# Second layer's feed-forward as two phases over DRAM with seven half-block products (Strassen) in place of eight

## The chip, the cores and the metric

One core of a Trainium2 chip runs the whole kernel. The metric is the device time of one execution in microseconds, the median of several runs. Engines: TensorE (PE, with its weight loads PEld), VectorE (DVE), ScalarE (ACT), GpSimd (POOL) and SyncE (SP), which issues all transfers of the stage in question in the order of its list.

## What is computed

A model of two layers, on 1024 tokens of 1024 features with 256 tokens of context, all in float32. Layer 0 mixes by neighbourhood attention and a gated linear recurrence, layer 1 by gated linear attention and grouped-query attention. Each layer ends in a feed-forward of width 4096, modulated by a conditioning vector; the last layer needs it for the 1024 latent tokens alone:

```python
D_FF = 4 * D_MODEL
...
def squared_relu_mlp(u, w1, w2):
    return jnp.square(jax.nn.relu(u @ w1)) @ w2
```

with `u` the normed and modulated residual, and its result times a gate added to the residual; the last norm follows.

## The kernel before

Activations lie feature-major: 128 features on the partitions, tokens along the free axis, in two chunks of 512 (c = 0, 1). TensorE's products keep float32 accuracy by splitting every operand into hi + lo (a rounding cast by ScalarE, the rest by a subtraction on VectorE or GpSimd, `split`) and adding three matmuls, hi hi, hi lo, lo hi, into one PSUM bank (`mm3`, L131 to L133). A matmul is 128x128 stationary by 128x512 moving.

The stage is `ff` (L1304) called for layer 1 at L2138. `ff_ops` lists its products: (1, g, c) makes the hidden blocks of group g, two blocks of 128 of the 4096 hidden features, for chunk c, 8 input tiles each, so 48 matmuls; (2, g, c) multiplies them by their rows of w2 into all eight output tiles, again 48 matmuls. In all 2 x 32 blocks x 8 tiles x 3, that is 1536 matmuls for each of the two layers, 3072 together, 128 x 512 all but the last few. First- and second-layer products of neighbouring groups alternate, so hidden never leaves SBUF. The first ones are (1, 0, 0), (1, 1, 0), (2, 0, 0), (1, 0, 1): two groups of chunk 0, then a second-layer product, and only then chunk 1, whose norm is still going on (`norm_mod` L1222, `mod_part` L348: VectorE scales, L354, ScalarE shifts and casts, L355, and VectorE, L363, or GpSimd, L361, takes the lo).

Per hidden block ScalarE applies Relu from PSUM (L1344), GpSimd squares (L1345), ScalarE casts hi (L138), VectorE takes lo (L139). Per output tile VectorE adds gate times PSUM to the residual `hl` in SBUF (L1363). Weights come in units of 128x1024, 512 KB each, by SyncE, some units ahead (`w_load`, `w_ahead`): ScalarE casts hi (L90), GpSimd subtracts lo (L92). The last product is done in two halves of the tokens, woven with the last norm (`final`, L2023), the transposes for it (L2032) and the stores (L2046).

Every engine runs its own list in order: an instruction that waits holds up all behind it. The list is what the Python program emits; generators (`fills`, stepped by `tick`) put background work between the products. SBUF tiles come from a pool of 45 slots of 4 KB a partition (`E.S`), six temporaries (`E.T`, `f`, `t`) and eight PSUM banks (`E.P`).

Of the kernel before, what the change touches and what calls it, by code (L numbers as in the profile page):

```python
# [366 lines left out]
def start(E):  # L367
    """x, ctx: row sums of squares, transposes, modulation and the norm of layer 0; x.T goes to DRAM."""
# [78 lines left out]
def col_units(key, ap, c0, n):  # L447
    """n units of 128 columns of a [1024, *] weight."""
# [12 lines left out]
def tick(E):  # L461
    """One step of every background generator."""
# [5 lines left out]
def store(E, dst, src, lag=4):  # L468
    """A store that is issued some background steps later, when its data is there."""
# [12 lines left out]
def pipe(gens, gap):  # L482
    """Software pipeline: a generator starts every gap steps, all started ones advance by one per step."""
# [54 lines left out]
def lru_tile(E, j, xl, gl, ct, o_d):  # L538
    """Conv, gates, both recurrences and the output gate of channels 128 j .. 128 j + 127."""
# [87 lines left out]
def na_bias_setup(E):  # L627
    """rpb rows padded to 127 columns in DRAM, so that a [64, 64] Toeplitz block is one strided read."""
# [14 lines left out]
def na_head_load(E, h, qk_d, v_d):  # L643
    """Bias tables and operands of head h."""
# [31 lines left out]
def na_head_mask(E, hd, i):  # L676
    """Quarter i of the masks of a head's bias tables."""
# [84 lines left out]
def run_attention(E, units, fill=None, lag=3):  # L762
    """Software pipeline over the units of an iterator: norm 1, turn lag, values lag + 1 steps after the scores."""
# [30 lines left out]
def attn_out(E, pair, parity, dst, flip=False):  # L794
    """dst[64 rows at 64 * parity, two query tiles] = the four partial products of pair.ps [128, 2, 2, 128], times pair.r."""
# [16 lines left out]
class Pair:  # L812
    """The outputs of two query tiles in PSUM, and 1 / sums along their columns; taken at the first use."""
# [152 lines left out]
def mixer0(E, u, st, tail):  # L966
    """st: what is left of the norm that writes u; tail(O, h): what follows chunk 2."""
# [124 lines left out]
class Back:  # L1092
    """The residual read back from DRAM: ctx() its chunk 2, lat() chunks 0 and 1 of 128 features more."""
# [29 lines left out]
def out_plan(E, l, w, early, late, cs):  # L1123
    """Weights of an out projection, 256 columns at a time: rows from 128 * early once per chunk, then the others."""
# [96 lines left out]
def norm_mod(E, h, u, c, gain, shift, pool=False, lag=2, which=0):  # L1221
    """u = norm(h) * gain + shift for chunk c, as a generator; the first eight steps take h.part(0..7)."""  # L1222
# [81 lines left out]
def ff(E, l, u, h, ops, G=2, fill=None, after=None, woven=False, slow=None, split=False):  # L1304
# [6 lines left out]
    hid, W = {}, {}  # L1311
# [12 lines left out]
    def ff1(g, c, outer):  # L1324
# [13 lines left out]
        for i in range(G):  # L1338
# [16 lines left out]
    def ff2_part(g, c, o, t0, n):  # L1355
        """128 features (o) of the product, for n tokens from t0 on of chunk c."""
# [8 lines left out]
    def ff2_end(g, c):  # L1365
        """The last product, half of the tokens after the other."""
# [51 lines left out]
    for i, (kind, g, c) in enumerate(ops):  # L1418
# [768 lines left out]
```

## Time and profile before

| | |
|---|---|
| median of three runs | 2994.42 us (2992.7 to 2995.53) |
| span of the profiled execution, its own time | 2993.8 us, 0.6 below the median |
| TensorE busy | 2898.8 us, 97% |
| VectorE, ScalarE, GpSimd busy | 54%, 40%, 36% |
| transfers | 286.98 MB, 96 GB/s in the mean |

Read it as one span on one core: the stage in question takes up its last quarter. Busy times are those of the whole span; what a stage is limited by has to be read from windows of it. A row of a timeline has the start, the busy time, the engine, the line of the program, the operation and its tiles.

### The profile page before, as it was taken

How to read it: one execution, taken by the hardware profiler on the slowest of the kernel's cores; microseconds unless marked ns; L12 is line 12 of the kernel's file. 1: busy time of each engine (PE TensorE's matmuls, PEld its weight loads, DVE VectorE, ACT ScalarE, POOL GpSimd, SP SyncE). 2: the span in 40 equal slices, each digit the busy share in tenths (PEclk: the TensorE clock that was granted, in tenths of full speed). 3: DMA queues.
4: the chain of work that ended last, by engine and by line, in shares of the span. 5: the costliest groups of instructions: out<-in, count | busy, mean ns of one | idle time of the engine just before them, and what ended most of it. 6: DMA issues, size and time to landing. Idle time of an engine off the chain costs nothing. (4 is left out here: it accounts for less than half of the span.)

```text
span 2993.8 us, 43072 instructions
## 1 busy us (share of the span) xinstructions
PE 2898.8 (97%) x16517; PEld 2500.8 (84%) x16517; DVE 1605.6 (54%) x3309; ACT 1195.7 (40%) x2301; POOL 1076.7 (36%) x866
## 2 busy tenths in 40 slices
PE   7999999989999999999999998899999999999998
PEld 5797789978888888888888797789988888888887
DVE  5454458877434534534437566888886332323334
ACT  5654458864211112112125343578884112112122
POOL 1443347643332222223234334325545233323230
PEclk9999999999999999999999999999999999999999
DMA  7235698831221221321213221334411111111111
GB/s 253 86 113 193 222 246 230 232 97 43 71 64 50 71 78 51 105 71 57 84 43 125 86 78 39 103 106 139 142 45 58 43 57 43 57 43 50 49 57 57
DMA packets 235173, 286.98 MB, mean 96 GB/s; under 512 B 32656, under 2 KB 172760, under 8 KB 234968
## 3 DMA queue, kind: packets, MB, share of 16 engines
q1 hardware_dynamic: 234968, 284.24, 30.9%
q8 instruction: 130, 2.13, 0.3%
q14 instruction: 75, 0.61, 0.1%
HBM read 226.97 MB, written 57.23 MB: 95 GB/s over the span
## 5 line engine op out<-in xcount | busy, mean ns | idle before, releaser
L131 PE MATMUL ps<-act,whi 128*128 128x512 f32 (+1 forms) x2176 | 805.1, 370 | 6.5 <-ACT act L355 5.4
L132 PE MATMUL ps<-act,whi 128*128 128x512 f32 (+1 forms) x2176 | 800.5, 368 | 0.8 <-POOL act L361 0.7
L133 PE MATMUL ps<-act,wlo 128*128 128x512 f32 (+1 forms) x2176 | 798.6, 367 | 2.1 <-POOL wlo L92 1.2
L92 POOL TENSOR_TENSOR wlo<-wst,whi 128x1024 fp32r<-128x1024 f32 x190 | 465.7, 2464 | 408.6 <-ACT whi L90 282.6
L139 DVE TENSOR_TENSOR hid<-t,hid 128x512 fp32r<-128x512 f32 (+1 forms) x160 | 102.3, 639 | 793.1 <-ACT hid L138 793.1
L131 PEld LDWEIGHTS ps<-act,whi 128*128 128x128 f32 x2176 | 412.9, 190 | 78.3 <-issue 7.4
L131 PE MATMUL ps<-hid,whi 128*128 128x512 f32 (+1 forms) x1296 | 476.2, 367 | 0.0
L132 PE MATMUL ps<-hid,whi 128*128 128x512 f32 (+1 forms) x1296 | 474.4, 366 | 0.0
L133 PE MATMUL ps<-hid,wlo 128*128 128x512 f32 (+1 forms) x1296 | 474.2, 366 | 0.0
L133 PEld LDWEIGHTS ps<-act,wlo 128*128 128x128 f32 x2176 | 412.0, 189 | 70.5 <-POOL wlo L92 1.6
L132 PEld LDWEIGHTS ps<-act,whi 128*128 128x128 f32 x2176 | 412.9, 190 | 65.5 <-POOL act L361 1.3
L1345 POOL TENSOR_TENSOR t<-t 128x512 f32<-128x512 f32 (+1 forms) x160 | 153.7, 960 | 865.6 <-ACT t L1344 857.5
L1344 ACT ACTIVATE t<-ps 128x512 f32<-128x512 f32 (+1 forms) x160 | 88.7, 555 | 922.2 <-PE ps L133 922.1
L1363 DVE SCALAR_TENSOR_TENSOR hl<-ps,mod,hl 128x512 f32<-128x512 f32 (+1 forms) x520 | 371.0, 738 | 134.3 <-PE ps L133 131.2
L131 PEld LDWEIGHTS ps<-hid,whi 128*128 128x128 f32 x1296 | 245.1, 189 | 41.6 <-issue 1.6
L133 PEld LDWEIGHTS ps<-hid,wlo 128*128 128x128 f32 x1296 | 245.0, 189 | 39.6
L132 PEld LDWEIGHTS ps<-hid,whi 128*128 128x128 f32 x1296 | 245.2, 189 | 38.9
L90 ACT CAST whi<-wst 128x1024 fp32r<-128x1024 f32 x194 | 197.9, 1048 | 82.9 <-PE ps L132 37.6
L723 ACT ACTIVATE sc<-sc,st 128x1024 f32<-128x1024 f32 (+3 forms) x208 | 178.1, 859 | 32.2 <-DVE st L1524 23.8
L752 DVE TENSOR_TENSOR pt<-ps,pt 128x512 fp32r<-128x512 f32 (+2 forms) x304 | 169.1, 598 | 18.9 <-ACT pt L751 16.4
L751 ACT CAST pt<-ps 128x512 fp32r<-128x512 f32 (+2 forms) x304 | 153.4, 526 | 37.2 <-PE ps L738 29.8
L138 ACT CAST hid<-t 128x512 fp32r<-128x512 f32 (+1 forms) x160 | 92.5, 578 | 184.3 <-POOL t L1345 184.3
(326 smaller groups left out, 4187.9 us busy)
## 6 DMA issues: line engine op xcount, KB each, us to landing
wst<-in_w_ff SPq DMA_DIRECT2D x128, 512.0 KB
wm<-in_w_mod SPq DMA_DIRECT2D x96, 512.0 KB
wst<-in_w_in_even SPq DMA_DIRECT2D x20, 512.0 KB
wst<-in_w_in_odd SPq DMA_DIRECT2D x18, 512.0 KB
qk_d<-qks SPq DMA_DIRECT2D x16, 512.0 KB
wst<-in_w_out_even SPq DMA_DIRECT2D x16, 512.0 KB
qst<-qk_d SPq DMA_DIRECT2D x32, 256.0 KB
he<-h_d SPq DMA_DIRECT2D x32, 256.0 KB
```

Source lines behind the costliest of these rows:

```text
L90: self.nc.scalar.copy(hi, st)
L92: engine.tensor_tensor(lo, st, hi.bitcast(F32), op=OP.subtract)
L131: t.matmul(ps, w[0], u[0], start=start, stop=False)
L132: t.matmul(ps, w[0], u[1], start=False, stop=False)
L133: t.matmul(ps, w[1], u[0], start=False, stop=stop)
L138: self.nc.scalar.copy(hi, src)
L139: (self.nc.gpsimd if pool else self.nc.vector).tensor_tensor(lo, src, hi.bitcast(F32), op=OP.subtract)
L723: self.E.nc.scalar.activation(s, s, AF.Exp, bias=self.nm, accum_out=self.st[:, 5 + i:6 + i])
L751: nc.scalar.copy(pt[:, :, 0], src)
L752: nc.vector.tensor_tensor(pt[:, :, 1], src, pt.bitcast(F32)[:, :, 0], op=OP.subtract)
L1345: nc.gpsimd.tensor_tensor(r, r, r, op=OP.mult)
L1363: nc.vector.scalar_tensor_tensor(dst, ps[:, :n], gate[:, o, v:v + 1], dst, op0=OP.mult, op1=OP.add)
```

## The change

The hidden features are divided: the first eighth (groups 0 and 1, four blocks) goes through both layers as before, but with hidden spilled to DRAM (`hid_d`) in between. The other 28 blocks are done in two phases. In the first, all of their hidden is made; in the second, it is all multiplied by w2. Each phase splits its two operands into half blocks and uses Strassen's seven products (in Winograd's form) in place of eight. Moving operands B (the halves of features by the two chunks) and their combinations are T1 = B12 - B11, T2 = B22 - T1, T3 = B22 - B12, T4 = B21 - T2; stationary ones are the weights' four quarters A and S1 = A21 + A22, S2 = S1 - A11, S3 = A11 - A21, S4 = A12 - S2.

- `ff_combine` makes T1 to T4 of the normed activations, 16 tiles, while the ordinary eighth runs; GpSimd sums hi + lo back to float32 (`whole`), VectorE subtracts, ScalarE casts, VectorE takes the lo. The residual is stored to DRAM meanwhile.
- `ff_first`: 14 pairs of hidden blocks, each seven products of 12 matmuls (four feature tiles of half the features, by three). The weight pieces (`block`) are cast by ScalarE, their lo is GpSimd's, s1, s2, a21, a12 are VectorE's. `post` combines three PSUM banks into four quarters, squares, makes T1 to T4 of the hidden, and stores all eight, 2 MB per pair.
- `ff_second`: 7 groups of four hidden blocks, each seven products of 24 matmuls, with operands read back from DRAM (`fetch`), the combinations of w2 made by VectorE and the residual read back.
- Then `ff` does the second layer of the first eighth, with the split end of before.

The lines of the new program stand one below those of before in most places (L139 for L138, L140 for L139).

```diff
-    ff_plan(E, 1, ops1)
+    ff_plan(E, 1, [(1, 0, 0), (1, 1, 0)])
...
-    ff(E, 1, u, h, ops1, fill=norm[1], after=lambda i: final(E, h, (2 * i, 2 * i + 1), fw), split=True)
+    ff_halves(E, 1, u, h, norm[1])
...
+def ff_halves(E, l, u, h, fill):
...
+    fills = [chain(fill, spill(), ff_combine(E, u, B))]
+    first = ff_first(E, l, B, pairs, {p: hs[p // 2][:, p % 2] for p in pairs}, fills)
+    ops = [(1, 0, 0), (1, 1, 0), (1, 0, 1), (1, 1, 1)]
+    ff(E, l, u, None, ops, fill=fills[0], spill=hd, rate=7)
+    drain(fills[0])
...
+    second = ff_second(E, l, groups, hs, residual, [])
...
+    ops = [(2, 0, 0), (2, 1, 0), (2, 0, 1), (2, 1, 1)]
+    ff(E, l, None, h, ops, after=lambda i: final(E, h, (2 * i, 2 * i + 1), fw), split=True, hid=hid)
...
+def ff_combine(E, u, B):
...
+    for a, b in ((T1, T2), (T3, T4)):
+        for k in range(4):
+            f12, f22 = whole(B[B12][k]), whole(B[B22][k])
+            yield
+            d = E.T([128, 512], name="ud")
+            if a == T1:
+                f11 = whole(B[B11][k])
+                nc.vector.tensor_tensor(d, f12, f11, op=OP.subtract)
+                nc.vector.tensor_tensor(f22, f22, d, op=OP.subtract)
+                yield
+                put(T1, d, False)
+                yield
+                put(T2, f22, False)
+            else:
+                f21 = whole(B[B21][k])
+                nc.vector.tensor_tensor(d, f22, f12, op=OP.subtract)
+                yield
+                put(T3, d, False)
+                nc.vector.tensor_tensor(f22, f32(B[T2][k], 0), f32(B[T2][k], 1), op=OP.add)
+                nc.vector.tensor_tensor(f21, f21, f22, op=OP.subtract)
+                yield
+                put(T4, f21, False)
+            yield
...
+    def post(d, bank):
...
+        v.tensor_tensor(g2[:, 1], bank.pop("z"), g2[:, 1], op=OP.add)
+        square(g2[:, 1])
+        yield
...
+        v.tensor_tensor(t1, b12, b11, op=OP.subtract)
+        v.tensor_tensor(t3, b22, b12, op=OP.subtract)
...
+        v.tensor_tensor(t2, b22, t1, op=OP.subtract)
+        v.tensor_tensor(t4, b21, t2, op=OP.subtract)
...
+def ff_second(E, l, groups, src, h, fills):
...
+    order = (1, 2, 6, 5, 3, 7, 4)
...
+            if n == 1:
+                a11, a21, a22, a12 = (raws.pop((i, m, z)) for m, z in ((0, 0), (0, 1), (1, 1), (1, 0)))
+                s1, s2, s4 = (E.S([128, 2, 512], name="ws") for _ in range(3))
+                v.tensor_tensor(s1, a21, a22, op=OP.add)
+                v.tensor_tensor(s2, s1, a11, op=OP.subtract)
+                v.tensor_tensor(a21, a11, a21, op=OP.subtract)
+                v.tensor_tensor(s4, a12, s2, op=OP.subtract)
...
+            w = pair(A.pop(n), True)
+            t = pair(moving.pop(j), j % 7 in (1, 3, 5))
...
+                first = n in (1, 6, 5, 7)
+                ps = E.P() if first else banks.pop(o)
```

How the order of the engines' lists moves, at three places. Before, GpSimd's list behind the last lo of chunk 1's norm (wlo: a weight's lo, t: the square of a hidden block):

```order
L92 TENSOR_TENSOR wlo4082_22907<-wst4051_22758,whi4081_22906 128x1024
L92 TENSOR_TENSOR wlo4084_22911<-wst4052_22760,whi4083_22910 128x1024
L1345 TENSOR_TENSOR t4086_22939<-t4086_22939 128x512
L1345 TENSOR_TENSOR t4091_22974<-t4091_22974 128x512
L1345 TENSOR_TENSOR t4102_23069<-t4102_23069 128x512
L1345 TENSOR_TENSOR t4105_23100<-t4105_23100 128x512
L92 TENSOR_TENSOR wlo4108_23107<-wst4088_22945,whi4107_23106 128x1024
L92 TENSOR_TENSOR wlo4110_23111<-wst4089_22947,whi4109_23110 128x1024
```

Now, at the end of the combinations (uf: a sum hi + lo, sw: the first weight pieces of the first Strassen pair):

```order
L1471 TENSOR_TENSOR uf4130_23076<-act4025_22609 128x512
L1471 TENSOR_TENSOR uf4133_23087<-act4067_22782 128x512
L1471 TENSOR_TENSOR uf4134_23089<-act4078_22836 128x512
L1471 TENSOR_TENSOR uf4136_23092<-act4030_22625 128x512
L140 TENSOR_TENSOR sw4143_23111<-wst4139_23103,sw4143_23111 128x512
L140 TENSOR_TENSOR sw4146_23118<-s4145_23115,sw4146_23118 128x512
L140 TENSOR_TENSOR sw4147_23121<-s4144_23114,sw4147_23121 128x512
```

All 24 sums stand ahead of the first weight piece. ScalarE's list there (ut: the hi of a combination T3 or T4, sw: a weight piece):

```order
L139 CAST ut4131_23079<-ud4129_23075 128x512
L139 CAST ut4132_23084<-uf4130_23076 128x512
L139 CAST ut4137_23095<-ud4135_23091 128x512
L139 CAST ut4138_23100<-uf4136_23092 128x512
L139 CAST sw4143_23111<-wst4139_23103 128x512
L139 CAST sw4146_23118<-s4145_23115 128x512
```

The first weight piece's hi stands behind the sixteenth combination's. ScalarE's list at the turn from the first phase to the second (sp: an operand of the second phase, hi; wr, ws: weights, hs: stored hidden, u: the kept first product, copied from PSUM):

```order
L139 CAST sp4415_25154<-wr4402_25059 128x1024
L139 CAST sp4417_25158<-hs4406_25067 128x1024
L1707 COPY u4429_25192<-ps4427_25178 128x512
L1707 COPY u4429_25192<-ps4428_25185 128x512
L1707 COPY u4432_25209<-ps4430_25194 128x512
L139 CAST sp4434_25213<-wr4405_25065 128x1024
L139 CAST sp4436_25217<-hs4407_25069 128x1024
L139 CAST sp4439_25223<-ws4412_25146 128x1024
L139 CAST sp4441_25227<-hs4414_25152 128x1024
```

The casts of the second product's operands, sp4434 and sp4436, stand behind three copies of the first product's results, where before ScalarE had weights' and hidden casts only. VectorE's list at the end of a group of the second phase (hl: residual, ws and wr: the next group's weights, sp: the lo of a moving operand; ps4527 is the fourth result of product 3, ps4541 the first of product 7):

```order
L1716 SCALAR_TENSOR_TENSOR hl4420_25164<-ps4525_25634,mod112_104,hl4420_25164 128x512
L1716 SCALAR_TENSOR_TENSOR hl4421_25166<-ps4526_25642,mod112_104,hl4421_25166 128x512
L1662 TENSOR_TENSOR ws4533_25696<-wr4502_25530,wr4503_25532 128x1024
L1663 TENSOR_TENSOR ws4534_25697<-ws4533_25696,wr4501_25528 128x1024
L1664 TENSOR_TENSOR wr4502_25530<-wr4501_25528,wr4502_25530 128x1024
L1665 TENSOR_TENSOR ws4535_25698<-wr4504_25534,ws4534_25697 128x1024
L140 TENSOR_TENSOR sp4540_25710<-hs4519_25616,sp4539_25709 128x1024
L1716 SCALAR_TENSOR_TENSOR hl4422_25168<-ps4527_25650,mod112_104,hl4422_25168 128x512
L1716 SCALAR_TENSOR_TENSOR hl4423_25170<-ps4541_25713,mod112_104,hl4423_25170 128x512
L1716 SCALAR_TENSOR_TENSOR hl4424_25172<-ps4542_25721,mod112_104,hl4424_25172 128x512
```

The four combinations of the next group's weights and one lo stand between the third and the fourth eviction of product 3, and ahead of product 7's; before, VectorE's evictions L1363 stood with nothing but a hidden block's lo (L139) between them.

## Rows read from the trace of the kernel before

**Rows 1.** Windows: busy time of each engine by stage, granted clock, DMA share, GB/s.

```profile
2322.00:2976.00 654.00, 654.00 (x2927) 542.93 (x2927) 221.38 (x321) 133.08 (x196) 196.54 (x117) 1.00 0.16 48
2976.00:2993.80 17.80, 9.86 (x78) 8.81 (x77) 11.39 (x28) 6.02 (x20) 0.00 (x0) 0.84 0.36 135
```

**Rows 2.** Waits of PE from 2279 to 2994 us: total, times, longest.

```profile
PE ps L2032 <- DVE hl L1363: 0.4, 1, 0.4
```

**Rows 3.** Timeline of PE where the stage begins.

```profile
2279.17 0.39 PE L131 MATMUL ps<-act,whi 128*128 128x512 f32 x1
...
2279.85 0.39 PE L131 MATMUL ps<-act,whi 128*128 128x512 f32 x1
```

**Rows 4.** Timeline of DVE, the norm of chunk 1.

```profile
2305.64 1.40 DVE L354 SCALAR_TENSOR_TENSOR t<-hl,gain,ps 128x512 f32<-128x512 f32 x2
...
2311.06 1.40 DVE L1363 SCALAR_TENSOR_TENSOR hl<-ps,mod,hl 128x512 f32<-128x512 f32 x2
...
2316.33 0.73 DVE L363 SCALAR_TENSOR_TENSOR act<-t,mod,act 128x512 fp32r<-128x512 f32 x1
2316.99 2.71 DVE L1363 SCALAR_TENSOR_TENSOR hl<-ps,mod,hl 128x512 f32<-128x512 f32 x4
```

**Rows 5.** Groups by line and shape, 2262 to 2994 us: count, busy, mean ns, idle before.

```profile
L1363 DVE SCALAR_TENSOR_TENSOR hl<-ps,mod,hl 128x512 f32<-128x512 f32 x248 | 179.9, 747 | 82.1 <-PE ps L133 82.1
L92 POOL TENSOR_TENSOR wlo<-wst,whi 128x1024 fp32r<-128x1024 f32 x63 | 149.9, 2403 | 50.2 <-ACT whi L90 48.1 <-DVE hl L1363 2.1
...
L1345 POOL TENSOR_TENSOR t<-t 128x512 f32<-128x512 f32 x64 | 66.6, 1040 | 394.8 <-ACT t L1344 394.8
...
L139 DVE TENSOR_TENSOR hid<-t,hid 128x512 fp32r<-128x512 f32 x64 | 44.3, 692 | 365.0 <-ACT hid L138 365.0
L138 ACT CAST hid<-t 128x512 fp32r<-128x512 f32 x64 | 39.7, 621 | 80.8 <-POOL t L1345 80.8
L1344 ACT ACTIVATE t<-ps 128x512 f32<-128x512 f32 x64 | 38.3, 598 | 437.5 <-PE ps L133 437.4
```

**Rows 6.** Timeline of POOL just ahead of the stage.

```profile
2275.06 2.42 POOL L92 TENSOR_TENSOR wlo<-wst,whi 128x1024 fp32r<-128x1024 f32 x1 [1.29 <-ACT whi L90]
2277.42 1.75 POOL L1232 TENSOR_TENSOR t<-t,t 128x512 f32<-128x512 f32 x1
2281.80 1.29 POOL L1232 TENSOR_TENSOR t<-t,t 128x512 f32<-128x512 f32 x1 [2.63 <-ACT t L1228]
```

**Rows 7.** Timeline of DVE over the same stretch as rows 6.

```profile
2275.56 2.46 DVE L363 SCALAR_TENSOR_TENSOR act<-t,mod,act 128x512 fp32r<-128x512 f32 x1
...
2278.60 1.12 DVE L363 SCALAR_TENSOR_TENSOR act<-t,mod,act 128x512 fp32r<-128x512 f32 x1
```

**Rows 8.** Instructions of lines L354 and L602 on DVE: ns min/median/max.

```profile
L354 DVE SCALAR_TENSOR_TENSOR t<-hl,gain,ps x48: 729/736/743, 700.0 to 2314.4; 128x512 f32<-128x512 f32 x48
L354 DVE SCALAR_TENSOR_TENSOR t<-hl,gain,rb x16: 737/746/2792, 38.1 to 69.6; 128x512 f32<-128x512 f32 x16
...
L602 DVE TENSOR_TENSOR lru<-lru,lru x8: 1225/1226/3236, 130.3 to 356.1; 128x1024 f32<-128x1024 f32 x8
```

**Rows 9.** Timeline and window of PE around its idle time at 362 us.

```profile
366.83 1.08 PE L302 MATMUL ps<-wm,cs 128*32 128x256 f32 x8 [4.47 <-DMA wm<-in_w_mod]
...
368.87 0.63 PE L133 MATMUL ps<-act,wlo 128*128 128x512 f32 x1
369.29 0.63 PE L131 MATMUL ps<-act,whi 128*128 128x512 f32 x1
...
365.00:370.00 5.00, 3.17 (x13) 1.97 (x14) 0.00 (x0) 0.00 (x0) 2.45 (x2) 0.66 0.99 347
```

**Rows 10.** Timeline of DVE from 135 us.

```profile
135.37 3.36 DVE L601 SCALAR_TENSOR_TENSOR lru<-lru,lru 128x1024 f32<-128x1024 f32 x1
138.84 3.24 DVE L602 TENSOR_TENSOR lru<-lru,lru 128x1024 f32<-128x1024 f32 x1
```

**Rows 11.** Timeline of POOL at the same time.

```profile
133.21 7.77 POOL L92 TENSOR_TENSOR wlo<-wst,whi 128x1024 fp32r<-128x1024 f32 x2 [15.01 <-PE ps L133]
```

More of the change, by code (lines that the diff above doesn't have):

```diff
@@ L1301, in ff_plan, with ff @@
             E.w_plan([((f"w{kind}", l, i), ap, shape)])
-def ff(E, l, u, h, ops, G=2, fill=None, after=None, woven=False, slow=None, split=False):
+def ff(E, l, u, h, ops, G=2, fill=None, after=None, woven=False, slow=None, split=False, hid=None, spill=None,
+       rate=0):
     nc = E.nc
     gate = E.mod[l][:, 5]
-    hid, W = {}, {}
+    hid, W, out = {} if hid is None else hid, {}, []
     fills = [fill] if fill is not None else []
@@ L1431, in ff, with whole, put @@
             pace = 0
-    return fills
+    for o in out:
+        nc.sync.dma_start(*o)
+    return fills
+FFA = 5
+FFB = 3
+B11, B21, B22, B12, T1, T2, T3, T4 = range(8)
+MOVING = {1: B11, 2: B21, 3: B22, 4: T4, 5: T1, 6: T2, 7: T3}
+def ff_combine(E, u, B):
+    nc = E.nc
+    for b, k, c in ((B11, 0, 0), (B21, 4, 0), (B12, 0, 1), (B22, 4, 1)):
+        B[b] = [u.tile(k + i, c) for i in range(4)]
+    for b in (T1, T2, T3, T4):
+        B[b] = []
+    f32 = lambda t, i: t[:, i].bitcast(F32)
+    def whole(t):
+        f = E.T([128, 512], name="uf")
+        nc.gpsimd.tensor_tensor(f, f32(t, 0), f32(t, 1), op=OP.add)
+        return f
+    def put(b, f, pool):
+        t = E.S([128, 2, 512], F32R, name="ut")
+        E.split(t[:, 0], t[:, 1], f, pool=pool)
+        B[b].append(t)
+    for a, b in ((T1, T2), (T3, T4)):
[11 more added lines that the diff above has]
+                put(T2, f22, False)
+            else:
+                f21 = whole(B[B21][k])
[7 more added lines that the diff above has]
+            yield
@@ new lines, in ff_first, with load, block, weights @@
+def ff_first(E, l, B, pairs, dst, fills):
+    nc = E.nc
+    raws, work = {}, []
+    def load(i):
+        if i < len(pairs):
+            p = pairs[i]
+            cols = E.A["w_ff1"][l][:, p * 256:p * 256 + 256].rearrange("(k p) o -> p k o", p=128)
+            raws[i] = (E.fp.tile([128, 4, 256], F32, name=E.nm("wst"), tag="ws"), E.S([128, 4, 256], name="wr"))
+            for h, t in enumerate(raws[i]):
+                nc.sync.dma_start(t, cols[:, 4 * h:4 * h + 4])
+    def block(src, pool):
+        t = E.S([128, 2, 4, 128], F32R, name="sw")
+        E.split(t[:, 0], t[:, 1], src, pool=pool)
+        return t
+    def weights():
+        v = nc.vector
+        for i in range(len(pairs)):
+            a, b = raws.pop(i)
+            a11, a21, a12, a22 = a[:, :, 0:128], a[:, :, 128:256], b[:, :, 0:128], b[:, :, 128:256]
+            load(i + 1)
+            yield block(a11, True)
+            s1, s2 = (E.T([128, 4, 128], name="s") for _ in range(2))
+            v.tensor_tensor(s1, a21, a22, op=OP.add)
+            v.tensor_tensor(s2, s1, a11, op=OP.subtract)
+            yield block(s2, True)
+            yield block(s1, True)
+            v.tensor_tensor(a21, a11, a21, op=OP.subtract)
+            del s1
+            yield block(a21, True)
+            yield block(a12, True)
+            del a, a11, a21
+            yield block(a22, True)
+            v.tensor_tensor(a12, a12, s2, op=OP.subtract)
+            del s2
+            yield block(a12, True)
+            del b, a12, a22
+    def square(t):
+        nc.scalar.activation(t, t, AF.Relu)
+        nc.scalar.activation(t, t, AF.Square)
+    def post(d, bank):
+        v = nc.vector
+        p1 = E.T([128, 512], name="p1")
+        nc.scalar.copy(p1, bank["x"])
+        yield
+        g2 = E.S([128, 2, 512], name="g")
+        v.tensor_tensor(g2[:, 1], bank["y"], p1, op=OP.add)
+        yield
+        yield
+        v.tensor_tensor(g2[:, 0], bank["y"], p1, op=OP.add)
+        v.tensor_tensor(g2[:, 0], bank["z"], g2[:, 0], op=OP.add)
+        square(g2[:, 0])
+        yield
+        g1 = E.S([128, 2, 512], name="g")
+        nc.scalar.activation(g1[:, 0], bank.pop("x"), AF.Relu)
+        nc.scalar.activation(g1[:, 0], g1[:, 0], AF.Square)
+        yield
+        v.tensor_tensor(g1[:, 1], bank.pop("y"), p1, op=OP.add)
+        del p1
+        square(g1[:, 1])
+        yield
+        v.tensor_tensor(g2[:, 1], bank.pop("z"), g2[:, 1], op=OP.add)
+        square(g2[:, 1])
+        yield
+        b11, b21, b22, b12 = g1[:, 0], g1[:, 1], g2[:, 0], g2[:, 1]
+        g3, g4 = (E.S([128, 2, 512], name="g") for _ in range(2))
+        t1, t2, t3, t4 = g3[:, 0], g3[:, 1], g4[:, 0], g4[:, 1]
+        v.tensor_tensor(t1, b12, b11, op=OP.subtract)
+        v.tensor_tensor(t3, b22, b12, op=OP.subtract)
+        nc.sync.dma_start(d[B11:B21 + 1].rearrange("i p t -> p i t"), g1)
+        yield
+        v.tensor_tensor(t2, b22, t1, op=OP.subtract)
+        v.tensor_tensor(t4, b21, t2, op=OP.subtract)
+        del g1, b11, b21, b12
+        yield
+        nc.sync.dma_start(d[B22], b22)
+        for o, g in ((T1, g3), (T3, g4)):
+            nc.sync.dma_start(d[o:o + 2].rearrange("i p t -> p i t"), g)
+        yield
+    load(0)
+    ws, ready, posts = weights(), [], []
+    order = ((1, "x"), (6, "y"), (5, "z"), (7, "y"), (2, "x"), (4, "y"), (3, "z"))
+    yield
+    for i, p in enumerate(pairs):
+        bank = {}
+        for j, (n, x) in enumerate(order):
+            while len(ready) < FFA:
+                w = next(ws, None)
+                if w is None:
+                    break
+                ready.append(w)
+            w = ready.pop(0)
+            first = x not in bank
+            if first:
+                bank[x] = E.P()
+            ms = B[MOVING[n]]
+            for k in range(4):
+                E.mm3(bank[x], (w[:, 0, k], w[:, 1, k]), (ms[k][:, 0], ms[k][:, 1]), first and k == 0, k == 3, not first)
+            del w, ms
+            if i == len(pairs) - 1:
+                del B[MOVING[n]]
+            posts = [g for g in posts if next(g, "end") != "end"]
+            if j == 0:
+                posts.append(post(dst[p], bank))
+            while fills and next(fills[0], "end") == "end":
+                fills.pop(0)
+            yield
+    while posts:
+        posts = [g for g in posts if next(g, "end") != "end"]
+        yield
```

152 lines of the change are left out of this document (144 added, 8 removed).

## The prediction

> **What bounds the kernel now.** Read the stage first, then TensorE's spacing, then the other engines, then the places where one of them was held up.
>
> From 2322 to 2976 us, nearly all of the second feed-forward, TensorE is busy for 654.00 of 654.00 us at the full granted clock, with VectorE at 34%, ScalarE at 20% and GpSimd at 30%; only the last 17.8 us are not TensorE's [rows 1]. In the whole stage its one wait on another engine is 0.4 us [rows 2]. Matmuls of 128x512 follow each other at 0.2267 us (three in 0.68) [rows 3], which is the full level, 2.4 GHz. So the stage costs as many matmuls as it has, and a matmul less is 0.2267 us less as long as nothing else comes between.
>
> **The change part by part.**
>
> *The saving.* TensorE's list falls from 13822 to 13486 rows: 2688 matmuls become 7/8 of that, 2352. 336 x 0.2267 = **-76.2 us**.
>
> *The operands of chunk 1.* Before, a second-layer product ran between chunk 0 and chunk 1 of the first layer and covered the rest of chunk 1's norm. Now chunk 1 follows at once, 4 blocks x 24 matmuls x 0.2267 = 21.8 us after the stage began, and its first block wants the eighth tile at 27. That norm's VectorE chain began at 2305.64 and ended at 2317.06, 26.4 and 37.9 us after the stage's begin at 2279.2; the four evictions in it (2 x 1.40) fall away and one lo of a hidden block, some 0.7, comes in [rows 4], which leaves 36. So TensorE waits up to 36 - 27 = 9; as the chain may begin a little sooner I take **+8** (0 to 10). The ordinary eighth, 43.5 us of matmuls, then ends at X = 52.
>
> *The combinations T1 to T4.* This is the part that decides. Nothing of the Strassen stage can start before them: GpSimd's order has the first weight piece behind all 24 sums, ScalarE's behind all 16 casts (the second and third list of the change). Casts of T1 stand behind the sixth hidden block's cast on ScalarE, at 6 x 5.44 + 8, and 0.60 + 1.04 + 0.62 for function, square and cast [rows 5] = 43. From there on eight steps (two combinations each) go through three engines: per step GpSimd 3 sums x 1.29 = 3.9 us [rows 6], VectorE 4 or 5 operations x 0.69 = 3.1, ScalarE 2 casts x 0.62. Do the first two overlap? The rows say hardly: VectorE's L363 takes 0.74 alone but 2.46 next to GpSimd's L92, GpSimd's next L1232 1.75 where it takes 1.29 alone, and VectorE's next 1.12 [rows 6, 7]. They take turns by whole instructions, and the records of a turn overlap by about 0.15. L354 with a PSUM operand never stretches (729 to 743 ns), with two in SBUF it reaches 2792 [rows 8]; and every VectorE operation of these steps has two SBUF operands. So a step costs between 3.9 (GpSimd alone) and 3.9 + 3.1 = 7.0; I take 6.5, for the overlaps. 8 x 6.5 = 52, so the last is there at 95; X was 52: TensorE stands for **+43** (8 x 3.9 = 31 gives +22, 8 x 7.0 = 56 with the first weight's cast and lo gives +49).
>
> The Trainium skill, "SBUF — State Buffer", section "Who interferes with whom", says that a VectorE instruction with two SBUF inputs contends with a GpSimd one that reads SBUF, and that whoever comes first holds the pair for the whole instruction. Taken strictly that makes the step 7.0 and the sum 4 us more than mine; the 0.15 of overlap in the rows is why I stay below it.
>
> *Clock after the gaps.* After TensorE had idled 4.47 us, the five next 512-column matmuls were 0.42 apart instead of 0.23, at a granted clock of 0.66 over those 5 us: the lower level, 1.2 GHz, for some 2 us, so about 1 us lost [rows 9]. Three long gaps (here and the two of the turn below) make **+3** (0 to 9, when the six small ones pay it also).
>
> *First phase, 14 pairs of 84 matmuls, 19.04 us each.* VectorE, ScalarE and GpSimd each have some 9 us of work in a pair, by 0.66 (four evictions in 2.71 [rows 4]) to 0.69, 0.62 and 1.29 for a 128x512 operation. Transfers are 1 MB of weights and 2 MB of combined hidden, 3 MB in 19 us, 165 GB/s, where 347 were moved in one window [rows 9]. I cost them at **0**; TensorE's own work covers them. If the first sum of a pair came late (I count it at 6.3 us, wanted at 8.2) it would be half a microsecond a pair: 0 to 7.
>
> *The turn between the phases.* VectorE must end the last pair: one sum from PSUM 0.66, ScalarE's two functions 1.2, four differences 2.8, one turn of GpSimd 2.4, 7.0 together. Then stand s1, s2, a21, s4 and the lo of the moving operand, five 128x1024 operations with two SBUF operands at 1.23 [rows 8], 6.2: product 1's second matmul waits 13. ScalarE's casts for product 2 stand behind three copies of product 1's results (the fourth list), and GpSimd then does two lo's of 2.40 [rows 5] before product 2: 5. **+18** (11, if the posts end while product 7 runs, to 25 with two more turns of GpSimd and the 4 MB residual late).
>
> *Second phase, 7 groups of 168 matmuls, 38.1 us.* Per group VectorE has 28 additions x 0.66 and 8 operations x 1.23 = 28 us, GpSimd 10 x 2.40 = 24: neither is the bound by sum, but they meet. VectorE's list has the next group's s1, s2, a21, s4 and a lo, 6.2 us, between two evictions, and TensorE's product 4 needs the bank that the eviction of product 7 behind them reads (the fifth list). They can start 0.7 us before product 7, which lasts 5.44; with two evictions behind them, 1.3, they end at 6.2 + 1.3 - 0.7 = 6.8, 1.2 to 1.4 late if nothing comes between. GpSimd is busy for 24 of 38, so I add one of its 2.40: 3.6. Six groups prepare a next one: **+21** (0, if the burst starts a block earlier, to 36 at 6 each).
>
> *The end.* 4 MB of hidden come back while the last group runs, then 192 ordinary matmuls with the split end as before: **+2** (0 to 5).
>
> Sum: -76.2 + 8 + 43 + 3 + 0 + 18 + 21 + 2 = **+18.8 us**. On the profiled execution's 2993.8 that is 3012.6; the median of the runs, 2994.42, is 0.6 above it, so 3013. All low ends together are -76.2 + 0 + 22 + 11 = -43, all high ones +65.
>
> **The rivals.** A measurement of this kernel tells about 0.2%, 6 us, from no change.
>
> *GpSimd's pace alone (faster).* If the sums on GpSimd and the differences on VectorE run beside each other, or the turns are short, a step of the combinations is 3.9: +22. The turn costs 11, a burst its 1.2: -76.2 + 8 + 22 + 3 + 11 + 7 + 2 = -23, so 2971. For it: GpSimd was 30% busy in this stage, and in steady stretches nobody waits [rows 1, 2]. Against it: [rows 6 to 8]. It decides from where a step of two combinations falls below 5 us.
>
> *Every operation of the burst meets another of GpSimd (slower still).* Three to four turns of 2.40 in place of one raise a burst to 6 and the turn to 25: -76.2 + 10 + 49 + 6 + 25 + 36 + 2 = +52, 3046. For it: in the stretch at 133 us two VectorE operations of 1.23 took 3.36 and 3.24 beside two L92 that lasted 7.77 [rows 10, 11]: every one was held. Against it: GpSimd's queue waits there for ScalarE's casts.
>
> *The gains and the waits meet (no change).* A combination step at 5.5, bursts at 2.4 and a turn of 14: -76.2 + 8 + 35 + 3 + 14 + 14 + 2 = 0, 2994.
>
> That the matmuls are not saved is excluded by the list; that transfers bound it, by 165 GB/s against 347.
>
> **How the numbers follow.** Combinations and bursts in turns, forecast 3013: 0.48. Slower still, 3046: 0.12. Faster, 2971: 0.30. No change: 0.10. So faster 0.30, within 0.2% 0.10, slower 0.60. The likeliest case alone is 3001 to 3030. The range must take in the faster rival with most of its own spread, and half of the slower: 2962 to 3042.
>
> **What would show it.** Right: TensorE without matmuls for about 43 us, some 52 us into the stage, its end released by ScalarE's or GpSimd's weight piece; VectorE's and GpSimd's records there stretched in turn; pairs of 19.0 us; about 18 us lost at the turn; six gaps of some 3.6 us before product 4. Wrong: a first gap under 30 us, VectorE's 512-column differences at 0.69 beside busy GpSimd, or pairs over 19.5 us.

## The result and the profile after

The changed kernel takes 3037.98 us (3036.59 to 3040.64, four runs) against 2994.49 before: ratio 1.0144, 95% interval 1.0129 to 1.0158, so 43 us slower, where 3013 was forecast. The profiled execution has a span of 3034.8 us, 41.0 more than before's 2993.8; what follows is measured on that.

Where TensorE waited for another engine, from 2270 us to the end (total, times, longest):

```profile
PE ps L132 <- ACT sw L139: 44.0, 1, 44.0
PE ps L132 <- DVE hl L1716: 23.1, 6, 5.9
PE ps L133 <- DVE sp L140: 7.9, 1, 7.9
PE ps L132 <- ACT sp L139: 5.2, 2, 4.0
PE ps L133 <- DVE act L364: 4.3, 1, 4.3
PE ps L133 <- POOL sp L140: 3.4, 1, 3.4
PE ps L133 <- POOL act L362: 1.1, 2, 0.6
```

Before there was one such wait, of 0.4 us [rows 2]. Line by line these are the forecast's places: the combinations T1 to T4 (44.0), the six bursts in the second phase (23.1; a burst is the row of operations that VectorE has between two evictions of PSUM banks), the turn between the phases (7.9 + 5.2 + 3.4 = 16.5) and chunk 1's late norm (4.3 + 1.1 = 5.4). Together they are 89.3 us with 0.3 of the first phase. But 89.3 - 76.2 is +13.1, and the kernel lost 41.0. The missing 28 stand in no wait. They show in the windows by stage, which are the gap before the first phase, the first phase, the turn and the second phase (busy of PE, PEld, DVE, ACT, POOL; granted clock; DMA share; GB/s):

```profile
2332.50:2376.90 44.40, 0.36 (x2) 0.00 (x0) 32.88 (x33) 10.68 (x18) 29.51 (x20) 0.54 0.21 71
2377.00:2638.00 261.00, 260.61 (x1140) 214.86 (x1141) 148.24 (x175) 124.87 (x215) 143.99 (x98) 0.99 0.44 147
2638.00:2680.00 42.00, 25.51 (x86) 19.40 (x85) 18.93 (x18) 18.65 (x25) 15.25 (x7) 0.76 0.78 295
2680.00:2968.00 288.00, 264.85 (x1101) 216.21 (x1100) 211.12 (x237) 89.38 (x91) 177.64 (x68) 0.93 0.40 136
```

The granted clock is 0.93 over the whole second phase, where it was 1.00 over 654 us of the stage before [rows 1]. TensorE's timeline at one of the six bursts shows how (start, busy, engine, line):

```profile
2790.89 0.39 PE L133 MATMUL ps<-sp,sp 128*128 128x512 f32 x1
2791.11 0.39 PE L134 MATMUL ps<-sp,sp 128*128 128x512 f32 x1
2794.94 0.77 PE L132 MATMUL ps<-sp,sp 128*128 128x512 f32 x1 [3.44 <-DVE hl L1716]
2795.50 0.63 PE L133 MATMUL ps<-sp,sp 128*128 128x512 f32 x1
2795.93 0.63 PE L134 MATMUL ps<-sp,sp 128*128 128x512 f32 x1
...
2799.77 0.63 PE L134 MATMUL ps<-sp,sp 128*128 128x512 f32 x1
2800.20 0.59 PE L132 MATMUL ps<-sp,sp 128*128 128x512 f32 x1
2800.62 0.40 PE L133 MATMUL ps<-sp,sp 128*128 128x512 f32 x1
2800.86 0.39 PE L134 MATMUL ps<-sp,sp 128*128 128x512 f32 x1
```

TensorE idles 3.44 us, and then 13 matmuls go at 0.43 us apiece, the lower level of 1.2 GHz, before they are back at 0.23: together 2.91 us more than at the full level. No row names it as a wait, since TensorE counts as busy. Adding up all spacings over 0.2267 us, without the idle times, gives for each place (us):

| place | forecast idle | measured idle | lost to the clock behind it |
|---|---|---|---|
| norm of chunk 1 | 8 | 5.4 | 3.4 |
| T1 to T4, with the first pair | 43 | 44.3 | 2.7 |
| first phase | 0 | (in the line above) | 0 |
| turn | 18 | 16.5 | 6.4 |
| six bursts | 21 | 23.2 | 15.5 |
| end | 2 | 0 | 0.2 |
| sum | 92 | 89.3 | 28.1 (forecast 3) |

-76.2 + 89.3 + 28.1 = +41.2, against 41.0 between the spans.

The turns of VectorE and GpSimd are there as well. In the gap of 44 us, VectorE's timeline and then GpSimd's:

```profile
2338.99 1.73 DVE L1486 TENSOR_TENSOR ud<-uf,uf 128x512 f32<-128x512 f32 x1 [2.38 <-POOL uf L1471]
2340.76 1.64 DVE L1487 TENSOR_TENSOR uf<-uf,ud 128x512 f32<-128x512 f32 x1
2342.32 1.75 DVE L140 TENSOR_TENSOR ut<-ud,ut 128x512 fp32r<-128x512 f32 x1
2343.99 0.68 DVE L140 TENSOR_TENSOR ut<-uf,ut 128x512 fp32r<-128x512 f32 x1
```

```profile
2334.81 8.71 POOL L1471 TENSOR_TENSOR uf<-act 128x512 f32<-128x512 f32 x6
```

While GpSimd sums, until 2343.52, three VectorE operations of 0.69 take 1.64 to 1.75; the fourth, with GpSimd done, takes 0.68. The six sums take 8.71 where they would take 6 x 1.29 = 7.7 alone. The steps for T3 and T4 (from one L1494 to the next) are 8.6, 6.6 and 6.1 us apart; 6.5 was taken. But turns are not all that is in them, as VectorE's timeline of the third one shows:

```profile
2366.12 0.68 DVE L1494 TENSOR_TENSOR ud<-uf,uf 128x512 f32<-128x512 f32 x1
2367.48 0.99 DVE L140 TENSOR_TENSOR ut<-ud,ut 128x512 fp32r<-128x512 f32 x1 [0.68 <-ACT ut L139]
2368.39 1.74 DVE L1497 TENSOR_TENSOR uf<-ut 128x512 f32<-128x512 f32 x1
```

VectorE waits here for ScalarE's cast of the tile whose lo it takes. Over the 44 us VectorE's records cover 32.7, where its 32 operations at 0.69 would be 22; so some 11 us, by this estimate, are GpSimd's turns. For 11.5 VectorE is idle, most of it in eight such waits of 0.68 for a cast, in 3.2 for the casts of two hidden blocks and in 2.4 for a sum.

And a burst:

```profile
2785.41 1.22 DVE L1662 TENSOR_TENSOR ws<-wr,wr 128x1024 f32<-128x1024 f32 x1
...
2788.94 1.22 DVE L1665 TENSOR_TENSOR ws<-wr,ws 128x1024 f32<-128x1024 f32 x1
2790.07 3.40 DVE L140 TENSOR_TENSOR sp<-hs,sp 128x1024 fp32r<-128x1024 f32 x1
2793.40 3.37 DVE L1716 SCALAR_TENSOR_TENSOR hl<-ps,mod,hl 128x512 f32<-128x512 f32 x5
```

Four combinations of 1.22, then one lo that takes 3.40 in place of 1.23, since GpSimd's lo (L140 from 2789.11) has come first: 1.2 of own work over the slack and one turn of 2.2, as forecast. In the first of the six bursts two operations met GpSimd, s1 with 3.15 and the lo with 3.37, and the wait was 5.95.

### The profile page after: what moved, and what is told of

The parts are those of the page before. It is cut to its first block, busy times and chain, and to the rows that moved or that the text cites. A ratio compares the mean times of both kernels' runs of the same rounds, so it can differ in the third digit from the quotient of the medians.

```text
span 3034.8 us, 43217 instructions
## 1 busy us (share of the span) xinstructions
PE 2848.8 (94%) x16181; PEld 2453.1 (81%) x16181; DVE 1837.2 (61%) x3507; ACT 1314.1 (43%) x2475; POOL 1250.3 (41%) x946
## 5 line engine op out<-in xcount | busy, mean ns | idle before, releaser
L132 PE MATMUL ps<-act,whi 128*128 128x512 f32 (+1 forms) x1728 | 630.9, 365 | 6.3 <-ACT act L356 5.2
L133 PE MATMUL ps<-act,whi 128*128 128x512 f32 (+1 forms) x1728 | 627.4, 363 | 6.2 <-DVE act L364 4.4
L134 PE MATMUL ps<-act,wlo 128*128 128x512 f32 (+1 forms) x1728 | 625.1, 362 | 2.1 <-POOL wlo L92 1.1
L92 POOL TENSOR_TENSOR wlo<-wst,whi 128x1024 fp32r<-128x1024 f32 x134 | 333.3, 2496 | 365.4 <-ACT whi L90 242.6
L132 PEld LDWEIGHTS ps<-act,whi 128*128 128x128 f32 x1728 | 329.2, 190 | 60.7 <-issue 7.6
L133 PEld LDWEIGHTS ps<-act,whi 128*128 128x128 f32 x1728 | 329.1, 190 | 55.3 <-DVE act L364 5.8
L140 DVE TENSOR_TENSOR hid<-t,hid 128x512 fp32r<-128x512 f32 (+1 forms) x104 | 65.5, 630 | 451.8 <-ACT hid L139 451.8
L132 PE MATMUL ps<-hid,whi 128*128 128x512 f32 (+1 forms) x848 | 301.2, 355 | 0.0
L133 PE MATMUL ps<-hid,whi 128*128 128x512 f32 (+1 forms) x848 | 299.6, 353 | 0.0
L134 PE MATMUL ps<-hid,wlo 128*128 128x512 f32 (+1 forms) x848 | 299.4, 353 | 0.0
L1372 DVE SCALAR_TENSOR_TENSOR hl<-ps,mod,hl 128x512 f32<-128x512 f32 (+1 forms) x296 | 208.7, 731 | 63.2 <-PE ps L134 60.1
L724 ACT ACTIVATE sc<-sc,st 128x1024 f32<-128x1024 f32 (+3 forms) x208 | 178.1, 859 | 32.1 <-DVE st L1826 23.1
L132 PE MATMUL ps<-sp,sp 128*128 128x512 f32 x392 | 161.5, 412 | 28.3 <-DVE hl L1716 23.1
L132 PEld LDWEIGHTS ps<-hid,whi 128*128 128x128 f32 x848 | 160.4, 189 | 24.0 <-issue 1.6
L134 PEld LDWEIGHTS ps<-hid,wlo 128*128 128x128 f32 x848 | 160.3, 189 | 22.1
L133 PEld LDWEIGHTS ps<-hid,whi 128*128 128x128 f32 x848 | 160.4, 189 | 21.5
L133 PE MATMUL ps<-sp,sp 128*128 128x512 f32 x392 | 160.1, 408 | 11.3 <-DVE sp L140 7.9
```

What stands on the lines that cost most here:

```text
L92: engine.tensor_tensor(lo, st, hi.bitcast(F32), op=OP.subtract)
L132: t.matmul(ps, w[0], u[0], start=start, stop=False, **kw)
L133: t.matmul(ps, w[0], u[1], start=False, stop=False, **kw)
L134: t.matmul(ps, w[1], u[0], start=False, stop=stop, **kw)
L140: (self.nc.gpsimd if pool else self.nc.vector).tensor_tensor(lo, src, hi.bitcast(F32), op=OP.subtract)
L724: self.E.nc.scalar.activation(s, s, AF.Exp, bias=self.nm, accum_out=self.st[:, 5 + i:6 + i])
```

## The experiments

Ten kernels ran; each batch ran beside the kernel before, whose median moved between 2995 and 2998, so ratios say more than differences of medians. Spans differ ahead of the stage too: the matmul behind TensorE's first wait in it starts at 2299.6 us in one profile and at 2311.3 in another, so what an edit is worth to a few us is read from the waits.

**Is the lost clock the echo of TensorE's idle time, or does the second phase's load bring it?**

```diff
+            if n == 4 and i < len(groups) - 1:
+                scratch = E.P()
+                for q in range(15):
+                    nc.tensor.matmul(scratch, w[0][:, q % 2, q // 2 % 4 * 128:q // 2 % 4 * 128 + 128], t[0][:, q % 2], start=True, stop=True)
+                del scratch
```

> Fifteen matmuls of 128x512 into a PSUM bank that nobody reads stand ahead of product 4 in six of the seven groups of the second phase, so TensorE works (15 x 0.2267 = 3.4 us) where it stood idle; nothing else is changed, and no result needs them. Theory (the lower clock is the echo of TensorE's idle time): the idle times before product 4 go (five of 3.44 to under 0.5, the first from 5.95 to about 2.5), their time is spent on the extra matmuls, but the 1.85 to 2.91 us lost after each at 0.43 us a matmul go: about 14 us less than the changed kernel's 3038, so 3024, granted clock 1.00 after the five. Rival (the clock falls for the second phase's own load, whatever TensorE did before): the low stretches stay, 3038 within 2.

It took 3024.03 us, ratio 1.0091 (1.0076 to 1.0106), where 3024 was expected; its span is 3023.4. The waits before product 4 are down to one, and at the place shown above TensorE now has:

```profile
2790.57 3.56 PE L1695 MATMUL ps<-sp,sp 128*128 128x512 f32 x15
2794.10 0.50 PE L132 MATMUL ps<-sp,sp 128*128 128x512 f32 x1
2794.44 0.40 PE L133 MATMUL ps<-sp,sp 128*128 128x512 f32 x1
```

Product 4 still has to wait as long, but then goes on at full rate: 0.24 us are lost behind each of the five, where it was 1.85 to 2.91. From 2720 to 2968 us TensorE is busy without a pause, at a granted clock of 1.00:

```profile
2720.00:2968.00 248.00, 248.00 (x1089) 203.84 (x1089) 192.10 (x221) 76.69 (x77) 147.21 (x57) 1.00 0.40 134
```

The span is 11.4 us less, though TensorE does nothing useful in the added matmuls. The theory holds: the load is not less, rather more, and the low level is gone. In the first of the six groups 2.54 us of idle time are left, and the low stretch behind them (1.9 us lost) stays.

**Is the burst one turn too long?** One number: the lo of product 1's moving operand moves to GpSimd.

```diff
-            t = pair(moving.pop(j), j % 7 in (1, 3, 5))
+            t = pair(moving.pop(j), j % 7 in (0, 1, 3, 5))
```

> The lo of product 1's moving operand goes from VectorE to GpSimd; it is the fifth operation of the burst, and the one that waited 2.2 us for GpSimd's turn (3.40 instead of 1.23). Theory (a gap is 1.2 of own work plus one turn, and the clock behind it): six gaps of 3.4 fall to under 0.5, and the low stretches behind them (15.5 us) go with them: 38 us less, 3000, some us less still at the turn. Rival (GpSimd with 26 of 38 us becomes late for product 1 or 2 of the next group): gaps move there, 3025 or more. Rival (the gap's price is the gap alone): 23 less, 3015.

It took 3005.81 us, ratio 1.0029 (1.0018 to 1.0041), where 3000 was expected; the span is 3001.5, 33.3 less than the changed kernel's. In the last five groups prepared no wait is left before product 4; two matmuls there come 0.36 us late together. In the first the wait stays, and is longer:

```profile
PE ps L132 <- DVE hl L1716: 8.0, 1, 8.0
```

VectorE's timeline says why:

```profile
2695.21 3.37 DVE L1664 TENSOR_TENSOR wr<-wr,wr 128x1024 f32<-128x1024 f32 x1
2698.51 3.37 DVE L1665 TENSOR_TENSOR ws<-wr,ws 128x1024 f32<-128x1024 f32 x1
```

GpSimd is still behind with the lo's of the first group and works without a pause from 2678 to 2704, so that all four combinations take 2.74 to 3.37 in place of 1.22. In this one place every operation of the burst does meet GpSimd. The other five are as the theory had it.

**Does spreading do the same?** s1 stays with product 1's operands; s2, a21 and s4 go to those of products 2, 6 and 5 (`if n == 2:` and so on around each).

> s1, s2, a21 and s4 of a group are no longer made together before product 1's operands: s1 stays there, s2 is made with the operands of product 2, a21 with those of product 6, s4 with those of product 5, each before it is needed. Theory: no place in VectorE's list has more than two such operations between evictions, so the six gaps go, with the clock behind them: 23 + 15.5 = 38 less; at the turn between the phases product 1 waits for one sum in place of four, 3.5 less and a smaller echo: about 42 to 46 less in all, 2992 to 2996. Rival (each operation takes its turn with GpSimd wherever it stands, 2.4 each time, and holds up an eviction there): gaps of 1 to 2 us in several products, 20 less at most, 3018.

It took 3012.93 us, ratio 1.0056 (1.0041 to 1.0071): between the theory's 2992 to 2996 and the rival's 3018. The waits before product 4 are gone but for 2.3 in the first group, and new ones of 1.36 to 1.49 stand at product 2, in six groups:

```profile
2801.95 0.47 PE L132 MATMUL ps<-sp,sp 128*128 128x512 f32 x1 [1.49 <-DVE u L1718]
2802.26 0.40 PE L133 MATMUL ps<-sp,sp 128*128 128x512 f32 x1
```

After 1.49 us of idle time the matmuls go on at full rate: 0.26 lost, not 2.9.

**Both edits together.**

> The two edits of the second phase together: the combinations of a group's weights spread over the operands of products 1, 2, 6 and 5, and the lo of product 1's moving operand on GpSimd. Theory: either alone left a rest that the other takes away (8.0 us in the first group where they stand together, 1.49 in six groups where the lo is VectorE's), so under 0.5 in each group: 23.2 idle and 15.5 clock less than the changed kernel, and 4 less at the turn: 2993 to 2998. Rival (GpSimd, 26 of 38 us now, becomes late for the products behind): gaps there, 3003 or more.

It took 3007.28 us, ratio 1.0039 (1.0026 to 1.0053): a miss, no better than the lo alone. The waits of 1.49 us stay. VectorE's timeline there:

```profile
2784.43 2.84 DVE L1670 TENSOR_TENSOR wr<-wr,wr 128x1024 f32<-128x1024 f32 x1
2787.19 3.41 DVE L140 TENSOR_TENSOR sp<-hs,sp 128x1024 fp32r<-128x1024 f32 x1
2790.53 0.74 DVE L1725 SCALAR_TENSOR_TENSOR hl<-ps,mod,hl 128x512 f32<-128x512 f32 x1
2791.19 1.87 DVE L1718 TENSOR_TENSOR u<-ps,u 128x512 f32<-128x512 f32 x3
```

a21 and product 6's lo now stand together, each with a turn of GpSimd, ahead of the evictions of product 1; and product 2 adds into product 1's banks. The spread had moved part of the burst from one pair of products that share banks (7 and 4) to another (1 and 2).

**Are the 44 us the turns, or the order of the lists?** One attempt gives them more cover, two eighths done in the ordinary way (`groups = list(range(2, 8))`, four hidden groups first, fewer background steps each):

> Two eighths of the hidden features are done in the ordinary way instead of one, chunk 1 comes after three groups of chunk 0, and the background work is spread over them. 6 groups in place of 7 use Strassen: 48 matmuls more, 10.9 us, and one gap less in the second phase (6.3 with its clock). Theory (the combinations take some 50 us from 43 us into the stage on, by turns of VectorE and GpSimd, wherever they stand): ordinary work now lasts 87 us, so they end at 92 to 100: the gap of 44 falls to 5 to 13, the start's 5.4 and 3.4 of clock go: about 40 less, 2994 to 3002. Rival (the order holds the combinations back, and they come the longer after the ordinary work the more of it there is): the gap stays at 30 or more, 3020.

It took 3032.97 us, ratio 1.0124 (1.0108 to 1.0141), where 2994 to 3002 was expected: a miss. The waits:

```profile
PE ps L132 <- DVE hl L1718: 24.8, 8, 5.8
PE ps L132 <- ACT sw L139: 18.0, 1, 18.0
PE ps L132 <- ACT whi L90: 13.5, 1, 13.5
```

44 becomes 18.0 and 13.5: the combinations now also hold up an ordinary weight, whose cast stands behind theirs on ScalarE. With 10.9 us of added matmuls nearly all is given back. The rival's 30 us or more remain (31.5), but the run says little between the two theories: the last 5.80 us of the 18.0 are ScalarE's wait for the transfer of the first weights, which neither of them had.

The other attempt takes GpSimd and the two-operand work away: TensorE makes the combinations.

```diff
+    def put(b, k, terms):
+        ps = E.P()
+        for j, (m, x) in enumerate(terms):
+            for z in range(2):
+                nc.tensor.matmul(ps, idp if m > 0 else idm, B[x][k][:, z], start=j + z == 0, stop=j == len(terms) - 1 and z == 1)
         t = E.S([128, 2, 512], F32R, name="ut")
-        E.split(t[:, 0], t[:, 1], f, pool=pool)
+        E.split(t[:, 0], t[:, 1], ps)
...
+        put(T2, k, ((1, B22), (-1, B12), (1, B11)))
```

> T1 to T4 of the activations are made by TensorE: for each of the 16 tiles 4, 6, 4 or 8 matmuls with the identity or its negative add hi and lo of the blocks in PSUM, 88 matmuls = 19.9 us; ScalarE casts hi from there, VectorE takes the lo with one operand in PSUM. GpSimd has no part in it, and no VectorE operation of it has two operands in SBUF. Theory (the gap of 44 is eight steps of GpSimd and VectorE in turns): it falls to 0 to 6, the 2.6 of clock behind it go if it does; 46.7 - 19.9 = 27 less, 3011 to 3017. Rival (it is the order of ScalarE's list, weight pieces behind 16 casts, and the late norm of chunk 1, not the turns): a gap of 15 or more remains, 3025 or more.

It took 3022.02 us, ratio 1.0089 (1.0075 to 1.0103), where 3011 to 3017 was expected. The gap of 44 is 7.4, though weight pieces still stand behind all 16 casts, so it was the combinations' own work and not the place of the weight pieces in ScalarE's list. Of the 7.4, 5.66 are another thing, as ScalarE's timeline shows; and a new wait came in, since TensorE's first use of the identity waited 3.4 for its cast behind a hidden block's lo:

```profile
2360.05 0.58 ACT L139 CAST ut<-ps 128x512 fp32r<-128x512 f32 x1
2366.29 0.62 ACT L139 CAST sw<-wst 128x512 fp32r<-128x512 f32 x1 [5.66 <-DMA wst<-in_w_ff]
```

The first weights' transfer is issued behind the last hidden store. How much of the 44 the turns made, and how much the number of operations and the waits for ScalarE's casts, this run does not separate: it took all of them away.

**Is the turn in-order waiting?** On the kernel with both edits, loads 7 products ahead, and products 1 and 2's operands split ahead of the last products:

```diff
+    for _ in range(2):
+        ready.append(next(ops))
+        yield
...
-        if left == 4:
+        if left in (7, 2, 1):
             next(second)
```

> The kernel of the two edits, and at the turn between the phases the second phase's first weights and operands are loaded 7 products ahead of the end instead of 4, and products 1 and 2's operands are split ahead of the last two products of the first phase, so ahead of the last pair's posts on VectorE and ahead of the copies of product 1's results on ScalarE. Theory (the turn is in-order waiting, 14 to 16 idle and 6 of clock behind the idle times): 5 or less remain, 12 to 15 less than the kernel of the two edits: 2980 to 2984. Rival (the operands' loads and the 4 MB residual bound the turn): 10 or more idle remain, 2990.

It took 3001.38 us, ratio 1.0023 (1.0014 to 1.0033). The turn's idle time falls from 12.1 us to 8.4 (0.2, 4.9, 1.5, 1.8), the clock behind it from 6.9 to 4.0, half of what was expected: product 6's lo on VectorE is now late, behind a21 and the last posts. All edits together:

> All of it together: TensorE makes T1 to T4, the combinations spread, the lo on GpSimd, the turn prepared. Theory (gaps and their echoes add up one by one): the kernel before, less 76.2, more 19.9 for the identities, 5.4 + 3.4 at the start, some 7 at the turn and 2 in the second phase: 2956 to 2962, 1.2% less than before. Rival (one wait taken away uncovers another): 2970 or more.

It took 2990.73 us, ratio 0.9984 (0.9975 to 0.9993). The rival was right on the size: the waits for the transfer (7.6), the identity (3.4) and product 1's banks (10.1) stayed. With those three mended:

> The kernel of all the edits with three changes. First, the identities are cast when the stage begins and not behind a hidden block's lo (3.38 idle and 1.75 of clock there). Second, the first weights of the first phase are asked for behind the last T4 and ahead of the last hidden store, not behind it (7.59 idle: ScalarE waited for that transfer, and 1.98 of clock). Third, of the four combinations and seven moving operands' lo of a group no two that VectorE makes stand together: s1, s2, s4 and a21 with the operands of products 2, 6, 5 and 7, the lo of products 2, 6, 5 and 7 on GpSimd, those of 1, 3 and 4 on VectorE. Theory (product 2 waited 1.49 for the bank of product 1 because a21 and a lo stood ahead of its eviction): the 1.49s go (six, 9 with the first's 2.65 and 1.6 of clock 14). In all 5 + 8 + 12, and 4 at the turn: 2962 to 2970. Rival (with one operation at each place every eviction is a turn of GpSimd late, and GpSimd at 26 of 38 us becomes the bound): 2975 or more, new idle times of 1 to 3 us at products 3 or 4.

It took 2973.27 us, ratio **0.9926** (0.9914 to 0.9939): 0.74% less than the kernel before, and between the theory's 2962 to 2970 and the rival's 2975. The 1.49s are gone; the longest waits that are left:

```profile
PE ps L132 <- DVE hl L1717: 11.2, 7, 4.2
PE ps L133 <- DVE act L364: 4.3, 1, 4.3
PE ps L132 <- ACT u L1708: 2.2, 2, 1.5
PE ps L132 <- ACT sw L139: 1.6, 1, 1.6
```

Nearly all of the 11.2 stands at the turn and in the last group. Over 260 us of the second phase TensorE is at 0.99 of its clock, with GpSimd busier (177.80 of 260, 68%) than in the changed kernel (62%):

```profile
2680.00:2940.00 260.00, 255.12 (x1120) 208.66 (x1119) 221.18 (x234) 79.81 (x88) 177.80 (x66) 0.99 0.38 128
```

The control has two operations together at another place (`j % 7 in (0, 1, 2, 5)` for `(1, 2, 3, 5)`):

> The same, but VectorE has the lo of product 5's moving operand, together with s4 (two operations with two SBUF operands at one place), and none with product 1's. Theory: two at that place delay evictions of products whose banks nobody waits for soon, so it is the same within 3 us; rival (two together always cost a gap): 1.5 in each of six groups, 9 more.

It took 2989.9 us, ratio 0.9979 (0.9970 to 0.9989), 16.6 more than the one without the pair. Six groups have a wait at product 2 again, 2.52 in the first and 2.11 in five. The rival was right that the pair costs a gap, and its 1.5 a group was too low:

```profile
2803.51 2.91 DVE L1660 TENSOR_TENSOR ws<-wr,ws 128x1024 f32<-128x1024 f32 x1
2806.34 3.42 DVE L140 TENSOR_TENSOR sp<-hs,sp 128x1024 fp32r<-128x1024 f32 x1
2809.69 0.68 DVE L1710 TENSOR_TENSOR u<-ps,u 128x512 f32<-128x512 f32 x1
```

s4 and the lo, each held by GpSimd, stand ahead of product 1's fourth eviction, and product 2's fourth part wants that bank.

## Why the prediction was right on the places and wrong on the sum

- *The saving*: right. 336 matmuls less, 0.2267 each where the clock is full; the first phase ran its 14 pairs (1176 matmuls) from 2376.9 to 2646.2 us, 269.3 against the 266.6 of 14 x 19.04; 0.3 of it is idle and the rest the clock behind the gap.
- *The combinations*: right in size (43 for 44.0), from 46 to 98 us into the stage for 43 to 95, and in mechanism in part. The turns are there in the stretched records of both engines. But they make some 11 of the 44 us, and VectorE's idle time another 11.5, for ScalarE's casts above all, which the sum took as covered; that a step of 6.5 came out (6.4 in the mean) is luck to that extent. The order of the lists, given as the reason why nothing could start before, was true but not the lever. The Trainium skill ("SBUF — State Buffer", "Who interferes with whom") says that a VectorE instruction with two SBUF inputs contends with a GpSimd one that reads SBUF. The stretched records agree, with 1.64 to 1.75 us for 0.69. Turns taken strictly gave the prediction 47, or 49 with the first weight's cast and lo; 44.0 was measured.
- *The bursts*: right, 3.44 in five of six (5.95 in the first, with two turns) for 3.6, with one turn of GpSimd. Moving one lo took five of them away.
- *The turn*: right, 18 for 16.5 (13 and 5 for 11.9 and 4.6). The start was taken as 8 for 5.4, the end as 2 for 0.
- *Clock after the gaps*: this is the step that failed. It read "about 1 us lost" from one row, a stretch where TensorE came back to the full level after five matmuls [rows 9], and "three long gaps ... make +3 (0 to 9)". Measured are 28.1 us. The row itself was read too low: a granted clock of 0.66 over 5 us is 1.7 us of full clock missing (0.34 x 5), and the eight small matmuls ahead of the five were slowed too (1.08 us, where the same eight took 0.64 ahead of the idle time). The price was short even so: behind the gaps of the changed kernel the low level lasted for up to 13 matmuls, and 1.9 to 3.4 us were lost at each place (6.4 at the turn's four gaps). The count was short too: the long gaps that were to make 3 pay 9.1, the start pays 3.4 and had no term, and the six bursts, put into the upper bound at 1 us each, pay 15.5. The Trainium skill ("TensorE: Matmul & The Clock Gate", Part 1) says that the slow clock is the default state, which activity releases. Behind the gaps of 3.4 us and more the traces agree, with 0.43 us a matmul; behind 1.49 us the matmuls go on at 0.23. That this is the idle time's echo, as the term had it, is shown by the run with 15 added matmuls; with the term at 28 the sum would have been +44, and the measured one is +43.
- The term's bounds went wrong with it: 9 as its high end came from the same one row. The signs that the prediction named came true, from the 44 us to the six gaps, because none of them looked at the clock.

Of the rivals, GpSimd's pace alone would have left a gap of 22; it was 44. That the gains and the waits meet asked for bursts of 2.4 and a turn of 14; they were 3.44 and 16.5. That every operation of a burst meets GpSimd happened in the changed kernel only in part: to one operation of five in five of the six bursts, to two in the first. The 3046 of that rival was near the time for another reason.

## What to carry to other kernels

A stall on TensorE has two prices: the wait, which the list of waits shows, and the low clock behind it, which no wait shows. Add the waits to the matmuls saved, compare that with the difference of the spans, and look for what is missing in the granted clock and in the spacing of matmuls behind each gap. Before an engine's work is spread or moved, note which eviction stands behind it and which product adds into that bank: two such operations (s1 and a lo) left no wait ahead of product 4 in five groups of the spread kernel, while two others (s4 and a lo, or a21 and a lo) ahead of an eviction of product 1 cost 2.1 or 1.5 us a group.

## What the runs showed of the hardware

How much clock an idle time costs, from a choice of the gaps of these kernels (idle before the first matmul, then what the matmuls behind lost against 0.2267 us each):

| idle, us | lost behind it, us |
|---|---|
| 0.58 | 0.3 |
| 1.49 to 1.51 (in four kernels) | 0.25 to 0.29 |
| 2.11 (five of them) | 0.28 or 0.29, once 1.80 |
| 2.29 (one in the spread kernel) | 1.87 |
| 2.52 (one in the control) | 0.29 |
| 2.65 | 1.6 to 1.8 |
| 3.44 (five in the changed kernel) | 1.85 to 2.91 |
| 7.94 (3.99 and one matmul ahead of it) | 2.6 to 3.0 |
| 44.0 | 2.2 to 2.4 |

A gap of 44 us costs no more clock than one of 3.4, so many stalls of 3.4 are dearer than one long one of the same sum. The same idle time does not always cost the same (2.11: 0.28 and 1.80; 2.29 cost more than 2.52), and in one burst the low level began 1.2 us after the matmuls did. The 15 extra matmuls that nobody reads gave back 11 us, nearly all of it at five of their six places, which is a remedy where a wait itself can't be taken away.
